# Two gate/up weight pairs instead of one take the two token halves apart in a SwiGLU channel mixer

## The chip, the cores and the metric

One core of one Trainium2 chip runs the whole program. Its engines are PE (matrix products), DVE (VectorE), ACT (ScalarE), POOL (GpSimd) and SP, which here only issues DMAs. The metric is device time in microseconds. Three runs of the kernel before took 3117.2, 3121.27 and 3121.76 us; the median is 3121.27.

## The reference

Two layers of a trunk run on 1152 tokens (128 context and 1024 sample tokens) of width 1024. Each layer is a token mixer followed by a dense SwiGLU channel mixer of hidden width 2816, both with adaptive scale, shift and gate:

```python
xs = xs + g1 * _token_mixer(_modulate(_rmsnorm(xs, norm1_g), sh1, sc1), ...)
xs = xs + g2 * _swiglu(_modulate(_rmsnorm(xs, norm2_g), sh2, sc2), w_gate, w_up, w_down)

def _swiglu(h, w_gate, w_up, w_down):
    return (jax.nn.silu(h @ w_gate) * (h @ w_up)) @ w_down
```

All of it is fp32. The change is in the channel mixer alone.

## The kernel before

Every fp32 product is made of three PE products of split operands: `hilo` (L212, L213) copies a tile to a rounded high part on ACT and subtracts it on POOL to get the low part; `mm3` (L227 to L229) multiplies high by high, high by low and low by high.

Gate and up products use a seven-product scheme on 2 x 2 blocks. The hidden width has 22 row tiles of 128, taken in 11 pairs; a pair has a gate and an up weight block. `gate_up` does one block with one half of the tokens (576 tokens in two columns of 288). Call that a **pass**: seven products of 12 matmuls of 128x288 each, in the order A11, A12, S2, S1, S3, S4, A22, with their sums on DVE (L1426). `prep_unit` readies the seven weight operands of a block: four loads of 256 KB (L204), and in the order A11, A12, A22, S1, S3, S2, S4 seven **splits** (a cast on ACT and a subtraction on POOL of 128x512 each), with four additions on DVE in between (L187, L190, L193, L196). The third product of a pass so needs the sixth split.

The tokens' operand is made by `half_apply` for one half at a time, in four **blocks**. In a block DVE scales eight or four column pieces (L1389), ACT adds the shift, DVE forms four differences `ht` (L1397 to L1400), ACT and POOL split them into `hth` and `htl` (one POOL subtraction of 128x1152), and ACT and DVE split the plain operands into `hx`, `hy`, `hz` (L1410, L1411). Half a (the later tokens) is ready when the mixer starts. Half b is not: its four blocks are done beside the first passes.

For that the first weight pair is taken with half a alone, the ten others with a and then b, and the first pair once more at the very end with half b alone, its weights loaded and split again. `units` in `mixer` is this list; `hidden` goes through it. In it, `prep[i][1]` is the making of the present weights, `nxt` that of the next block's, one step after most products (seven steps in seven products where a unit has one half), and `side` is work beside it: `half_apply` of half b in the first unit, with a block after the third and the sixth product of each pass, and `g_load` of the first tiles for the down projection in the last one. When a pass of `up` is done DVE multiplies it into the gate's result (L1482) and SP writes it to DRAM (`gd`). `DOWN` lists in which groups of row tiles the down projection reads them back.

The engines' orders come from a scheduler that is given the code in this order; each engine runs its own list in order, and waits for others by semaphores. The products sit in eight PSUM buffers.

Of the kernel before, what the change touches and what calls it, by code (L numbers as in the profile page):

```python
# [34 lines left out]
NH = 8  # L35
HID = 22
NP = HID // 2
DOWN = ((2, 3, 4, 5, 6), (7, 8, 9, 10, 11), (12, 13, 14, 15), (16, 17, 18, 19, 20), (21, 0, 1))
CORD = (2, 1, 0)
EPS = 1e-6  # L40
SCALE = 96.0 ** -0.5
# [35 lines left out]
class Net:  # L77
# [39 lines left out]
    def order(self):  # L117
        q = []
        for l in range(L):
            q += [("in", l, i) for i in range(len(IN_FM))]  # L120
            q += [("woa", l, m) for m in range(8)] + [("wob", l, j) for j in range(2)]
            q += [("wo", l, m) for m in range(8)]
            q += [("dn", l, g, m) for g in list(range(len(DOWN))) + [len(DOWN) - 1] for m in range(KD)]
        self.queue = q
        self.qpos = 0

    def wsrc(self, key):
# [10 lines left out]
        if k == "dn":  # L138
            n = len(DOWN[key[2]]) * P
            c = sum(map(len, DOWN[:key[2]])) * KD * P + key[3] * n  # L140
            return a["w_down"][l, :, c:c + n], n
# [1309 lines left out]
    def hidden(self, l, hs, units, prep, beside, gd):  # L1451

        nc = self.nc
        prods = [(u, n) for u in range(len(units)) for n in ("gate", "up")]
        g = {}
        for i, (u, n) in enumerate(prods):
            p, halves = units[u]
            W, nxt = prep[i][0], prep[i + 1][1] if i + 1 < len(prods) else iter(())  # L1460
            side = beside.get(u, iter(()))
            t = 0
            for _ in prep[i][1]:
                pass
            next(nxt, None)
            for H in halves:
                for o in self.gate_up(W, hs[H], i == 0):
                    if o is not None:
                        break
                    t += 1  # L1470
                    if len(halves) == 1 or t not in (1, 3, 6, 8, 10, 12, 14):
                        next(nxt, None)
                    if t % 3 == 0 or u:
                        next(side, None)
                if n == "gate":
                    nc.scalar.activation(o, o, AF.Silu)
                    g[H] = o
                    continue
                v = g.pop(H)
                for jj in range(2):  # L1480
                    s = slice(2 * jj, 2 * jj + 2)
                    nc.vector.tensor_tensor(v[:, s], v[:, s], o[:, s], op=ALU.mult)  # L1482
                if p not in gd:
                    gd[p] = self.tc.dram_tile([P, 2, T], F32, name=self._nm("gd"))
                if H == 0:
                    w = v.rearrange("p (j c) n -> p j c n", j=2)
                    for t0, n0, p0 in ((0, 64, 0), (128, 224, 64)):
                        for jj in range(2):
                            d = gd[p][:, jj, t0:t0 + 2 * n0].rearrange("p (c n) -> p c n", c=2)
                            nc.sync.dma_start(out=d, in_=w[:, jj, :, p0:p0 + n0])  # L1490
                else:
                    nc.sync.dma_start(out=gd[p][:, :, 576:1152], in_=v.rearrange("p (j c) n -> p j (c n)", j=2))
            if n == "up":
                for _ in side:
                    pass
            if i == len(prods) - 2:
                self.prep_next()
# [14 lines left out]
    def down(self, l, x, xd, gd, first, out):  # L1512

        g = first
        for gi in range(len(DOWN) - 1):
            nxt = []
            ld = self.g_load(gd, DOWN[gi + 1], nxt, ())
            for m in range(KD):
# [14 lines left out]
        def tail():  # L1533
            for cs in (CORD[:1], CORD[1:]):
                for m in range(KD):
                    w = self.get(("dn", l, len(DOWN) - 1, m), ahead=1 if cs[0] == CORD[0] or m < KD - 2 else 0)
                    for c in cs:
# [14 lines left out]
    def mixer(self, l, x, o_tail):  # L1552


        a, b = HORDER
        sa, sb = [], []
        for _ in zip(o_tail(a), self.half_sq(x, a, sa)):
            pass
        hs = {a: [], b: []}
        qb = self.half_sq(x, b, sb)  # L1560
        units = [(0, (a,))] + [(p, (a, b)) for p in range(1, NP)] + [(0, (b,))]
        prep = []
        for p, _ in units:
            for n in ("gate", "up"):
                W = {}
                prep.append((W, self.prep_unit(l, n, p, W)))
        ga = None
        for m, _ in enumerate(o_tail(b)):
            next(prep[0][1], None)
            if m == 0:  # L1570
                ya = self.half_rsq(a, sa)
                ga = self.half_apply(l, x, a, ya, hs[a])
            else:
                next(ga, None)
            next(qb)
        for _ in qb:
            pass
        yb = self.half_rsq(b, sb)
        xd = self.tc.dram_tile([P, KD, T], F32, name=self._nm("xmid"))
        for k in range(KD):  # L1580
            self.nc.sync.dma_start(out=xd[:, k, :], in_=x[k])
        gd = {}
        first = []
        ld = self.g_load(gd, DOWN[0], first, CORD)
        self.hidden(l, hs, units, prep, {0: self.half_apply(l, x, b, yb, hs[b]), len(units) - 1: ld}, gd)
        x = [self.S("x") for _ in range(KD)]
        if l + 1 < L:
            self.side = self.ada_work(l + 1, range(3))
        return x, self.down(l, x, xd, gd, first, self.o["yT"] if l == L - 1 else None)
# [197 lines left out]
```

## Time and profile before

| | before |
|---|---|
| median of three runs | 3121.27 us |
| the profiled execution | 3115.68 us |
| its span, first to last instruction | 3113.8 us |
| mean granted TensorE clock | 0.987 |
| PE busy | 97% |
| DVE / POOL / ACT busy | 55% / 38% / 36% |

A span of 3113.8 us lies within the 3115.68 us of that execution; 1.9 us lie around it. The busy shares are means over stages. Tables by stretch show where PE is not full, and lists of waits show what ended each idle time. PEclk is the granted clock as a share of 2.4 GHz; 0.50 is 1.2 GHz.

### The profile page before, as it was taken

The numbers are of one execution on the slowest core, as the hardware profiler recorded it, in microseconds if no ns is written. First come the engines' busy times: TensorE is split into PE (matmuls) and PEld (weight loads), VectorE is DVE, ScalarE is ACT, GpSimd is POOL, SyncE is SP. The second block draws the span as 40 slices with busy tenths as digits, with TensorE's granted clock in tenths as the row PEclk, the third lists the DMA queues.
The fourth block names the chain that finished last, engine by engine and source line by source line (L and its number), as shares of the span: only waits on it lengthen the run. The fifth ranks groups of instructions, "written<-read, shape, count | busy, mean of one in ns | idle before, by whom it ended". The sixth has DMA issues, their size and how long they took to land.

```text
span 3113.8 us, 48728 instructions
## 1 busy us (share of the span) xinstructions
PE 3016.3 (97%) x19136; PEld 2678.3 (86%) x19136; DVE 1708.1 (55%) x3315; ACT 1131.7 (36%) x2734; POOL 1185.4 (38%) x780
## 2 busy tenths in 40 slices
PE   6999999999799999999999999999988999999999
PEld 5989855569799999988999897554888999999999
DVE  6264467658855455643272645667578555556343
ACT  4334465444422222321153335654444222223211
POOL 3111254565644343311242113445656343434212
PEclk9999999999899999999999999999999999999999
DMA  5323000032222222566231110011232122216223
GB/s 214 103 88 132 25 17 30 32 117 99 79 85 72 69 73 86 192 245 239 65 115 49 46 36 13 13 54 59 73 129 68 60 85 83 68 63 234 92 71 100
DMA packets 126725, 278.06 MB, mean 89 GB/s; under 512 B 24096, under 2 KB 47392, under 8 KB 126496
## 3 DMA queue, kind: packets, MB, share of 16 engines
q1 hardware_dynamic: 126496, 274.95, 26.1%
q8 instruction: 151, 2.47, 0.3%
q14 instruction: 78, 0.64, 0.1%
HBM read 222.57 MB, written 52.33 MB: 88 GB/s over the span
## 4 chain that ended last, share of the span: by engine, by line
PE 85%; DVE 9%; ACT 2%; DMA 2%; issue 1%; POOL 1%; SPq 0%; DVEq 0%; POOLq 0%; ACTq 0%
PE mm L227 14%; PE mm L229 14%; PE mm L228 14%; PE ax L227 6%; PE ax L228 6%; PE ax L229 6%; PE ax L1136 5%; PE ax L1107 3%; PE mm L1153 2%; PE mm L1154 2%; PE mm L1155 2%; PE ax L325 1%; PE ax L1096 1%; DVE hb L1389 1%; DVE hy L1411 1%
## 5 line engine op out<-in xcount | busy, mean ns | idle before, releaser
L213 POOL TENSOR_TENSOR W<-r,W 128x512 fp32r<-128x512 f32 x336 | 448.9, 1348 | 539.3 <-ACT W L212 524.4
L213 POOL TENSOR_TENSOR W<-W,W 128x640 fp32r<-128x640 f32 (+5 forms) x168 | 297.9, 1775 | 841.4 <-ACT W L212 496.2
L227 PE MATMUL mm<-gh,W 128*128 128x384 f32 x1056 | 354.7, 336 | 1.4 <-DVE u L1426 1.3
L229 PE MATMUL mm<-gh,W 128*128 128x384 f32 x1056 | 353.4, 335 | 0.9 <-POOL W L213 0.9
L228 PE MATMUL mm<-gl,W 128*128 128x384 f32 x1056 | 352.9, 334 | 0.0
L1271 DVE SCALAR_TENSOR_TENSOR x<-mm,mod,x 128x128 f32<-128x128 f32 (+2 forms) x320 | 158.1, 515 | 332.5 <-PE mm L229 332.5
L229 PE MATMUL ax<-hth,W 128*128 128x288 f32 x1056 | 315.5, 299 | 10.3 <-POOL W L213 10.3
L227 PE MATMUL ax<-hth,W 128*128 128x288 f32 x1056 | 315.5, 299 | 7.4 <-ACT W L212 7.4
L228 PE MATMUL ax<-htl,W 128*128 128x288 f32 x1056 | 314.8, 298 | 0.0
L1145 POOL TENSOR_TENSOR W<-W,W 128x1024 f32<-128x1024 f32 x96 | 232.5, 2422 | 169.9 <-ACT W L1156 163.5
L212 ACT CAST W<-W 128x640 fp32r<-128x640 f32 (+5 forms) x168 | 131.6, 784 | 388.8 <-DMA W<-in_w_down 176.1
L212 ACT CAST W<-r 128x512 fp32r<-128x512 f32 x336 | 205.4, 621 | 183.8 <-DMA r<-in_w_up 64.2
L1109 DVE TENSOR_REDUCE mx<-ax 128x1 f32<-128x384 f32 x384 | 194.4, 550 | 120.4 <-PE ax L1107 119.1
L227 PE MATMUL mm<-hh,W 128*128 128x384 f32 x704 | 239.8, 341 | 0.0
L229 PE MATMUL mm<-hh,W 128*128 128x384 f32 x704 | 238.6, 339 | 0.0
L1156 ACT ACTIVATE W<-mm 128x512 f32<-128x512 f32 x288 | 168.2, 606 | 191.1 <-PE mm L1155 187.4
L228 PE MATMUL mm<-hl,W 128*128 128x384 f32 x704 | 237.0, 337 | 0.0
L229 PEld LDWEIGHTS ax<-hth,W 128*128 128x128 f32 x1056 | 201.9, 191 | 11.4 <-POOL W L213 11.4
L227 PEld LDWEIGHTS ax<-hth,W 128*128 128x128 f32 x1056 | 201.8, 191 | 8.3 <-ACT W L212 8.3
L227 PEld LDWEIGHTS mm<-gh,W 128*128 128x128 f32 x1056 | 198.2, 188 | 12.2 <-issue 10.1
L1136 PE MATMUL ax<-W,vt 128*64 128x512 f32 x576 | 206.8, 620 | 0.0
L228 PEld LDWEIGHTS ax<-htl,W 128*128 128x128 f32 x1056 | 201.9, 191 | 0.0
(335 smaller groups left out, 7789.5 us busy)
## 6 DMA issues: line engine op xcount, KB each, us to landing
W<-in_ada_w SPq DMA_DIRECT2D x80, 512.0 KB, 5.0
gr<-gd SPq DMA_DIRECT2D x44, 576.0 KB, 5.3
r<-in_w_gate SPq DMA_DIRECT2D x96, 256.0 KB, 2.9
r<-in_w_up SPq DMA_DIRECT2D x96, 256.0 KB, 4.1
W<-in_w_in_fm SPq DMA_DIRECT2D x30, 512.0 KB, 3.7
W<-in_w_down SPq DMA_DIRECT2D x48, 320.0 KB, 3.5
gd<-gu SPq DMA_DIRECT2D x22, 576.0 KB, 3.7
gd<-gu SPq DMA_DIRECT2D x44, 224.0 KB, 2.2
```

What stands on the lines that cost most here:

```text
L212: self.nc.scalar.copy(hi, raw)
L213: self.nc.gpsimd.tensor_tensor(lo, raw, hi.bitcast(F32), op=ALU.subtract)
L227: self.nc.tensor.matmul(ps, wh, xh, start=first and i == 0, stop=False)
L228: self.nc.tensor.matmul(ps, wh, xl, start=False, stop=False)
L229: self.nc.tensor.matmul(ps, wl, xh, start=False, stop=last and i == n - 1)
L1107: nc.tensor.matmul(ps, qh[0:96, qt * P:(qt + 1) * P], kh[0:96, c * CH:(c + 1) * CH], start=True, stop=True)
L1109: nc.vector.reduce_max(mx[:, qt, c:c + 1], ps, axis=AX.X)
L1136: nc.tensor.matmul(po[64 * qc:64 * qc + 64, :], vv[:, kt, b:b + 64], prs[kt][:, qs], start=(kt == 0), stop=(kt == 8))
L1145: nc.gpsimd.tensor_tensor(acc, acc, prs[kt], op=ALU.add)
L1153: nc.tensor.matmul(ps, kh[0:104, ks], qh[0:104, qs], start=True, stop=False)
L1156: nc.scalar.activation(pr[:, qs], ps, AF.Exp, scale=SCALE)
L1271: self.nc.vector.scalar_tensor_tensor(x[m][:, t0:t1], ps[:, t0 - c * CH:t1 - c * CH], self.mod[l][:, j, m, i:i + 1], x[m][:, t0:t1], ALU.m ...
```

## The change

The second pair of row tiles is treated like the first: half a alone at the beginning, half b alone at the end. The mixer then has two single-half units at either end instead of one. The blocks of `half_apply` for half b are spread over both first units: one after the third product of each of the four passes, instead of two in each of two passes. `DOWN` is rearranged so that the tiles which are finished last are read last.

```diff
-DOWN = ((2, 3, 4, 5, 6), (7, 8, 9, 10, 11), (12, 13, 14, 15), (16, 17, 18, 19, 20), (21, 0, 1))
+DOWN = ((4, 5, 6, 7, 8), (9, 10, 11, 12, 13), (14, 15, 16, 17), (18, 19, 20, 21, 2), (3, 0, 1))
...
-                    if t % 3 == 0 or u:
+                    if t == 3 or u > 1:
                         next(side, None)
...
-            if n == "up":
+            if n == "up" and beside.get(u + 1) is not side:
                 for _ in side:
                     pass
...
-        units = [(0, (a,))] + [(p, (a, b)) for p in range(1, NP)] + [(0, (b,))]
+        units = [(0, (a,)), (1, (a,))] + [(p, (a, b)) for p in range(2, NP)] + [(0, (b,)), (1, (b,))]
...
+        late = self.half_apply(l, x, b, yb, hs[b])
         first = []
         ld = self.g_load(gd, DOWN[0], first, CORD)
-        self.hidden(l, hs, units, prep, {0: self.half_apply(l, x, b, yb, hs[b]), len(units) - 1: ld}, gd)
+        self.hidden(l, hs, units, prep, {0: late, 1: late, len(units) - 1: ld}, gd)
```

What this does to POOL's list in layer 0: here is the kernel before, from the second pass of the first unit on. `htl` is the subtraction of a block of half b, `W` a split of weights (the `r` that it reads is a weight load).

```order
L213 TENSOR_TENSOR htl_7553<-ht_7547,hth_7552 128x1152
L213 TENSOR_TENSOR W_7682<-r_7581,W_7682 128x512
L213 TENSOR_TENSOR W_7701<-r_7580,W_7701 128x512
L213 TENSOR_TENSOR htl_7660<-ht_7654,hth_7659 128x1152
L213 TENSOR_TENSOR W_7719<-r_7581,W_7719 128x512
L213 TENSOR_TENSOR W_7763<-r_7579,W_7763 128x512
L213 TENSOR_TENSOR W_7809<-r_7770,W_7809 128x512
L213 TENSOR_TENSOR W_7840<-r_7771,W_7840 128x512
L213 TENSOR_TENSOR W_7858<-r_7773,W_7858 128x512
L213 TENSOR_TENSOR htl_7742<-ht_7736,hth_7741 128x1152
```

And this is the changed kernel from the same (second) block of half b on.

```order
L213 TENSOR_TENSOR htl_7634<-ht_7628,hth_7633 128x1152
L213 TENSOR_TENSOR W_7692<-r_7555,W_7692 128x512
L213 TENSOR_TENSOR W_7710<-r_7553,W_7710 128x512
L213 TENSOR_TENSOR W_7742<-r_7717,W_7742 128x512
L213 TENSOR_TENSOR W_7759<-r_7718,W_7759 128x512
L213 TENSOR_TENSOR W_7776<-r_7720,W_7776 128x512
L213 TENSOR_TENSOR W_7821<-r_7720,W_7821 128x512
L213 TENSOR_TENSOR htl_7799<-ht_7793,hth_7798 128x1152
L213 TENSOR_TENSOR W_7840<-r_7719,W_7840 128x512
L213 TENSOR_TENSOR W_7858<-r_7720,W_7858 128x512
L213 TENSOR_TENSOR W_7876<-r_7718,W_7876 128x512
L213 TENSOR_TENSOR W_7905<-r_7880,W_7905 128x512
```

Before, two and five splits stand between the second, third and fourth `htl`; now six stand between the second and the third, and seven (not all shown) between the third and the fourth: one whole weight block per block of tokens.

At the other end of the mixer, this is SP's list in the kernel before, at the last two-half pair; `r` are weight loads, `gd` writes of finished halves, `gr` reads for the down projection.

```order
L1492 DMA gd_12509<-gu_12152 256x1x576
L1504 DMA gr_12658<-gd_8135 128x1152
L204 DMA r_12630<-in_w_up 128x512
L204 DMA r_12631<-in_w_up 128x512
L204 DMA r_12632<-in_w_up 128x512
L204 DMA r_12633<-in_w_up 128x512
L1490 DMA gd_12509<-gu_12269 128x2x64
```

The changed kernel has at that place the following, from the last write of that pair's half b on.

```order
L1490 DMA gd_12298<-gu_12058 128x2x224
L204 DMA r_12555<-in_w_gate 128x512
L204 DMA r_12556<-in_w_gate 128x512
L204 DMA r_12557<-in_w_gate 128x512
L204 DMA r_12558<-in_w_gate 128x512
L1504 DMA gr_12724<-gd_8410 128x1152
L204 DMA r_12696<-in_w_up 128x512
L204 DMA r_12697<-in_w_up 128x512
```

The loads of the additional pair (gate, then up) stand behind that pair's writes, and the first read for the down projection stands between them.

## Rows read from the trace of the kernel before

**Rows 1.** The page: PE's busy time; a group's count, busy us, mean ns
```profile
PE 3016.3 (97%) x19136; PEld 2678.3 (86%) x19136; DVE 1708.1 (55%) x3315; ACT 1131.7 (36%) x2734; POOL 1185.4 (38%) x780
...
L212 ACT CAST W<-r 128x512 fp32r<-128x512 f32 x336 | 205.4, 621 | 183.8 <-DMA r<-in_w_up 64.2
```

**Rows 2.** Busy time by stretch; columns in the first line
```profile
core 0: us, PE busy (x) PEld busy (x) DVE busy (x) ACT busy (x) POOL busy (x), PEclk, DMA share, GB/s
775.00:850.00 75.00, 57.62 (x368) 55.86 (x367) 66.11 (x137) 37.57 (x64) 50.19 (x32) 0.84 0.26 88
1000.00:1200.00 200.00, 200.00 (x1508) 200.00 (x1507) 102.92 (x180) 54.62 (x90) 80.59 (x64) 1.00 0.24 79
2300.00:2400.00 100.00, 83.24 (x556) 81.29 (x556) 85.04 (x168) 48.21 (x81) 64.69 (x39) 0.88 0.21 73
```

**Rows 3.** PE's waits, 770 to 860 us: total us, times, longest
```profile
PE ax L249 <- DVE sq L416: 6.7, 1, 6.7
PE ax L229 <- POOL W L213: 5.6, 2, 2.9
PE ax L227 <- ACT W L212: 3.8, 2, 3.2
PE mm L228 <- DVE hz L1411: 1.0, 1, 1.0
```

**Rows 4.** PE's waits in layer 1, 2290 to 2400 us
```profile
PE ax L229 <- POOL W L213: 4.7, 2, 2.7
PE ax L227 <- ACT W L212: 3.6, 2, 3.2
```

**Rows 5.** PE in order of time: start, duration, [idle before, releaser]
```profile
807.59 0.61 PE L229 MATMUL ax<-hth,W 128*128 128x288 f32 x1 [2.68 <-POOL W L213]
...
829.96 0.61 PE L229 MATMUL ax<-hth,W 128*128 128x288 f32 x1 [2.88 <-POOL W L213]
...
842.48 0.40 PE L228 MATMUL mm<-hz,W 128*128 128x288 f32 x1 [1.01 <-DVE hz L1411]
```

**Rows 6.** Busy time by stretch, around half b's blocks
```profile
804.00:812.80 8.80, 5.88 (x25) 5.65 (x26) 8.80 (x14) 6.14 (x12) 8.80 (x6) 0.64 0.27 90
...
822.70:833.00 10.30, 4.27 (x19) 4.00 (x20) 10.30 (x19) 6.23 (x12) 7.58 (x4) 0.70 0.08 27
795.00:846.00 51.00, 40.65 (x267) 39.46 (x267) 50.48 (x89) 29.90 (x49) 38.00 (x22) 0.87 0.16 54
```

**Rows 7.** ACT: first product of two successive passes taken over
```profile
862.62 0.40 ACT L1429 COPY u<-ax 128x288 f32<-128x288 f32 x1 [6.88 <-PE ax L229]
...
873.78 0.40 ACT L1429 COPY u<-ax 128x288 f32<-128x288 f32 x1 [3.32 <-PE ax L229]
```

**Rows 8.** DVE and POOL by line, 1000 to 1200 us: busy us, mean ns
```profile
L193 DVE TENSOR_TENSOR r<-r,r 128x512 f32<-128x512 f32 x9 | 15.9, 1768 | 15.6 <-POOL W L213 15.6
...
L196 DVE TENSOR_TENSOR r<-r,r 128x512 f32<-128x512 f32 x9 | 6.1, 679 | 0.0
...
L213 POOL TENSOR_TENSOR W<-r,W 128x512 fp32r<-128x512 f32 x64 | 82.8, 1304 | 119.5 <-ACT W L212 115.9 <-DMA r<-in_w_up 1.7 <-POOL W L213 1.2
```

**Rows 9.** By tile, whole span: duration ns min/median/max
```profile
L213 POOL TENSOR_TENSOR htl<-ht,hth x16: 2657/2835/3210, 743.6 to 2377.7; 128x1152 fp32r<-128x1152 f32 x16
...
L1399 DVE TENSOR_TENSOR ht<-hb x16: 444/446/2655, 740.6 to 2375.6; 128x288 f32<-128x288 f32 x16
...
L1482 DVE TENSOR_TENSOR gu<-gu,gu x88: 746/758/2833, 826.0 to 2839.1; 128x576 f32<-128x576 f32 x88
```

**Rows 10.** End of the mixer: SP, POOL and PE in order of time
```profile
1265.31 2.41 SPq L204 DMA_DIRECT2D r<-in_w_up  x4
1274.19 2.64 SPq L1490 DMA_DIRECT2D gd<-gu  x4
...
1282.37 2.65 POOL L213 TENSOR_TENSOR W<-r,W 128x512 fp32r<-128x512 f32 x2 [1.28 <-ACT W L212]
...
1296.81 0.42 PE L227 MATMUL mm<-gh,W 128*128 128x384 f32 x1 [0.64 <-DVE u L1426]
```

## The prediction

> **What bounds the kernel now.** Start with the page: PE is busy for 97% of the span [rows 1], so a change that adds no PE work can only fill PE's idle times or make new ones. The table by stretch shows where they are. In the middle of the channel mixer PE is busy for 200.00 of 200 us at the full clock; at its start it has 57.62 of 75 us at a granted clock of 0.84 in layer 0, and 83.24 of 100 at 0.88 in layer 1 [rows 2]. PE's list of waits for that start tells what ended each one [rows 3]. 6.7 us is for the norm of half b, which stands ahead of the first pass and is not touched. 5.6 + 3.8 us is for splits of weights and 1.0 for half b's last plain operand, together 10.4 us in layer 0; layer 1 has 4.7 + 3.6 us for splits [rows 4]. So about 20 us of waits are aimed at.
>
> In order of time [rows 5] these fall behind each other: third product of the second pass at 807.59, third product of the third pass at 829.96, and half b's operand at 842.48. In the stretches with the two longer ones the clock is 0.64 and 0.70 on the mean [rows 6], so part of each ran at 1.2 GHz.
>
> Now who is late. From 795 to 846 us DVE is busy for 50.48 of 51 us and POOL for 38.00 [rows 6], while PE is not. Part of DVE's time is itself waiting: in the undisturbed middle, L193 takes 1768 ns and L196, of the same size, 679 [rows 8]. L193 starts when POOL goes from S1's split to S3's, and the additional 1.1 us is most of that 1.30 us split. L1399 of 444 ns took up to 2655, L1482 of 746 up to 2833 [rows 9]. A DVE operation on two SBUF tiles and a POOL split take turns here.
>
> **What the change removes and adds.** PE's products are the same in number and size. Removed is the crowding of two blocks of half b into each of two passes. Added are two weight blocks per layer (gate and up of the second pair, a second time), each four loads, seven splits and four DVE additions; and two of the first four passes' blocks must now be ready within one pass, not two.
>
> What is not removed: on DVE and POOL the order is the same up to the end of the first block, and the 807.59 wait ends with the split behind that block's `htl`. It stays, in both layers.
>
> I compare one mark: the start of the third product of the fifth pass, when as much PE work is done in both kernels. Before, the sixth pass's first product was taken over at 862.62 and the next one's at 873.78 [rows 7]; a pass is 11.16 us and a product 1.59, so the mark is 862.62 - 11.16 + 1.59 = 853.05.
>
> In the changed kernel the mark waits for the sixth split of the fifth pass's weights. Behind 807.59 POOL's order has until there 21 splits (one left of the second pass, seven, seven and six) and three `htl`: 21 x 1.30 + 3 x 2.66 = 35.3 us [rows 8, 9]. DVE has, on two SBUF tiles, 11 weight additions at 0.68 = 7.5, 12 `ht` at 0.445 = 5.3, two gate-by-up halves at 0.76 = 1.5, and the low parts of `hx`, `hy`, `hz`: by the sizes 0.45, 0.75, 1.05 and 0.45 = 2.7 [rows 8, 9] (the 864 columns by the slope between 288 and 576). That is 17.0, and 52.3 with POOL's.
>
> How strictly do they take turns? The same count for the kernel before from 807.59 to 842.48, that is 11 splits, three `htl`, 5 additions, 12 `ht`, the low parts with a second 576 piece, and the two halves, gives 22.3 + 13.7 = 36.0 us against 34.9 measured, 0.97. So 52.3 x 0.97 = 50.7, and the mark comes at 858.3: 5.2 us later.
>
> The Trainium skill, "SBUF — State Buffer", section "Who interferes with whom", states it as a rule: a DVE instruction with two inputs in SBUF contends with a GpSimd instruction that reads SBUF, and the one issued second is blocked until the first is done. Taken strictly (the 52.3 without a factor) that rule puts the mark at 859.9, 1.6 us beyond the measured share; it speaks against this change, since the change adds work of both kinds ahead of the mark.
>
> Following the handoffs one at a time with the same durations (DVE's in-order list, with its waits for PE's third product in each pass) I get the third pass's third product at about 823 instead of 829.96, the fourth's at 840 where before it was 842, and the mark at 855.5. The early gain is eaten because a pass with one block and one weight block takes POOL and DVE some 15 to 17 us and PE 11.16. Between 855.5 and 858.3 I take 857: **4 us later per layer**. Layer 1 has the same waits, so 8 us in all.
>
> Bounds. Below: if turns cost nothing, POOL's 35.3 us and per weight block the addition and cast of 0.69 + 0.62 us between A22 and S1 [rows 1, 8] make 807.59 + 35.3 + 3 x 1.31 = 846.8, 6.3 us sooner. Above: 858.3 and the same 3.9 is 862.2, and if PE is then at 1.2 GHz for 6 us, 3 us more (around 807.59 the mean of 0.64 over 8.8 us is 6.3 us at that level [rows 6]): 12 us later. For two layers that is -13 to +24.
>
> The end of the mixer I cost at nothing. One more single-half unit makes POOL's splits due every 11.16 us instead of every 22.3, 7 x 1.30 = 9.1 us of work. Before has one such pair of passes already and only 0.64 us of wait there [rows 10]. Cover: the loads of the additional pair stand behind four writes that took 2.64 us to issue at 1274.19; the earlier such loads at 1265.31 had their sixth split done by 1283.7 [rows 10], 18.4 us. From 1276.9 that is 1295.3, and it is needed two passes and two products after the pass that ended at about 1274, so at 1299.5. The cover is 4 us for gate and, since the next block's third load waits for a split of the block ahead, some 3 us for up. The new `DOWN` reads nothing that is not long written.
>
> **The sum.** Span 3113.8 + 8 = 3121.8; device time 3115.68 + 8 = 3123.7. The profiled execution is 5.6 us below the runs' median, so 3121.27 + 8 gives **3129**.
>
> **Rivals.** *Turns do not bind.* With half b's blocks apart, DVE's operations could fall into POOL's gaps. For it: POOL was idle for 13 of the 51 us [rows 6]. Against: the 0.97. In full it gives the lower bound, 6.3 us per layer, with up to 1.5 us of clock saved, 3106 to 3109; in part, up to 3115. *A wait for a wait.* The third pass's gain and the later loss cancel, mark at 851 to 855: 3117 to 3125. For it: the handoffs alone gave 855.5. *Late weights at the end.* If the last loads take 5 us longer than that cover was counted with, up's third product waits 2 us in either layer, and the clock may fall, 3 us more: 8 + 2 x (2 + 3) = +18, 3139. For it: the loads are behind the writes and a 576 KB read. It decides once the loads take over 3 us longer than at 1265. Against: before, the same pattern left 0.64 us.
>
> **Chances.** 0.2% is 6.2 us, about what a measurement of this kernel tells from none. My forecast's case (mark 855 to 862, +3 to +18) has 0.52, of which 0.17 lies under 6.2; turns that do not bind 0.17; a wait for a wait 0.20; late weights 0.11. So faster 0.17, same 0.37, slower 0.46. The range that holds 8 in 10 is 3113 to 3141: it leaves out the far part of the first rival and of the last.
>
> **What would show it.** Right: the 2.7 us wait at 807.59 unchanged; three waits for splits behind it, of 2 to 4 us, at third products of the third, fourth and fifth pass, where before were two and `hz`'s; no wait for `hz`; DVE over 95% busy for 45 us; no wait for splits over 1 us at the mixer's end. Wrong: waits for splits that sum to under 6 us per layer, with POOL's gaps filled and L1399 or L1482 at their shortest durations; or waits at the end.

## The result, and the profile after

The changed kernel takes 3148.37 us (median of 4 runs, 3147.44 to 3153.28) against 3120.12 us before: a ratio of 1.0095, 95% interval 1.0083 to 1.0106, so 28 us slower, clear of noise. Forecast were 3129 and a range up to 3141: the sign was right, the size was not. The profiled execution has a span of 3151.5 us.

First, the page, as in [rows 1]: PE, POOL's total, and the splits, which now come 28 times more.

```profile
PE 3035.3 (96%) x19136; PEld 2691.8 (85%) x19136; DVE 1731.5 (55%) x3331; ACT 1145.7 (36%) x2762; POOL 1222.7 (39%) x808
...
L212 ACT CAST W<-r 128x512 fp32r<-128x512 f32 x364 | 221.1, 621 | 221.8 <-DMA r<-in_w_up 65.2
```

Busy time by stretch, with columns as in [rows 2]: the middle is untouched; in the start PE is idle for 25 of 100 us in layer 0 and for 25 of 130 in layer 1.

```profile
775.00:875.00 100.00, 74.54 (x475) 72.16 (x473) 82.40 (x157) 45.20 (x79) 67.98 (x43) 0.86 0.24 83
1000.00:1200.00 200.00, 200.00 (x1508) 200.00 (x1507) 100.37 (x179) 55.58 (x91) 80.20 (x63) 1.00 0.22 72
2300.00:2430.00 130.00, 104.86 (x666) 102.48 (x665) 107.37 (x189) 58.98 (x99) 88.49 (x52) 0.84 0.25 86
```

PE's waits from 770 to 870 us, the answer to [rows 3]. Waits for POOL's splits went from 5.6 to 13.6 us; half b's last operand is no longer waited for; a wait for `x` of 3.3 us stands where before was 0.3, and that for half b's norm is 5.2 instead of 6.7.

```profile
PE ax L229 <- POOL W L213: 13.6, 4, 4.5
PE ax L249 <- DVE sq L416: 5.2, 1, 5.2
PE mm L227 <- DVE x L1317: 3.3, 2, 3.0
PE ax L227 <- ACT W L212: 3.3, 3, 1.4
```

The same in order of time, as in [rows 5], with the end of the mixer:

```profile
779.23 0.37 PE L227 MATMUL mm<-hx,W 128*128 128x288 f32 x1 [3.00 <-DVE x L1317]
...
809.87 0.41 PE L229 MATMUL ax<-hth,W 128*128 128x288 f32 x1 [2.69 <-POOL W L213]
...
827.05 0.61 PE L229 MATMUL ax<-hth,W 128*128 128x288 f32 x1 [2.76 <-POOL W L213]
...
846.57 0.61 PE L229 MATMUL ax<-hth,W 128*128 128x288 f32 x1 [4.51 <-POOL W L213]
...
864.01 0.40 PE L229 MATMUL ax<-hth,W 128*128 128x288 f32 x1 [3.61 <-POOL W L213]
...
1309.69 0.66 PE L227 MATMUL mm<-gh,W 128*128 128x384 f32 x1 [2.49 <-DVE u L1426]
```

PE runs 19136 instructions in both kernels, and only their order in the mixer differs, so the start times of the instruction with the same number can be set against each other. The table is worked out so. "x" is PE's 4200th to 4300th (13750th to 13900th in layer 1), which takes in the wait for `x` and that for half b's norm; "start" goes on to the 4760th (14380th), beyond the fifth pass's third product; "middle" to the 7900th (17500th); "end" to the 8060th (17660th). All in us. The changed kernel was run a second time later, and its two traces are both given.

| stretch | before, layers 0 and 1 | after, first trace | after, second trace | mean difference of a layer |
|---|---|---|---|---|
| x | 21.9, 30.7 | 24.9, 33.8 | 26.2, 32.6 | +3.1 |
| start | 78.9, 79.4 | 86.8, 91.8 | 88.5, 88.3 | +9.7 |
| middle | 417.2, 414.5 | 417.2, 414.5 | 417.2, 414.5 | 0.0 |
| end | 25.1, 26.5 | 28.3, 29.7 | 28.4, 29.7 | +3.2 |

That is 16.0 us a layer, 32 for both. The timed difference is 28.2; the kernel before's profiled execution lies 4.4 us below its median, which is about the rest. In the start, waits are 6.7 us of the 9.7 (16.8 against 10.1 on the mean). The clock makes the remaining 3: the granted clock was at its lower level, 1.2 GHz, for 22 us of that stretch on the mean, against 16 before.

### The profile page after: what moved, and what is told of

It is laid out like the page before. It is cut to its first block, busy times and chain, and to the rows that moved or that the text cites. A ratio compares the mean times of both kernels' runs of the same rounds, so it can differ in the third digit from the quotient of the medians.

```text
span 3151.5 us, 48878 instructions
## 1 busy us (share of the span) xinstructions
PE 3035.3 (96%) x19136; PEld 2691.8 (85%) x19136; DVE 1731.5 (55%) x3331; ACT 1145.7 (36%) x2762; POOL 1222.7 (39%) x808
## 3 DMA queue, kind: packets, MB, share of 16 engines
q1 hardware_dynamic: 128800, 279.14, 26.2%
## 5 line engine op out<-in xcount | busy, mean ns | idle before, releaser
L213 POOL TENSOR_TENSOR W<-r,W 128x512 fp32r<-128x512 f32 x364 | 486.0, 1351 | 529.9 <-ACT W L212 521.1
L212 ACT CAST W<-r 128x512 fp32r<-128x512 f32 x364 | 221.1, 621 | 221.8 <-DMA r<-in_w_up 65.2
L227 PEld LDWEIGHTS mm<-gh,W 128*128 128x128 f32 x1056 | 199.2, 189 | 16.6 <-issue 14.4
```

Of the source, the lines that this page charges most:

```text
L212: self.nc.scalar.copy(hi, raw)
L213: self.nc.gpsimd.tensor_tensor(lo, raw, hi.bitcast(F32), op=ALU.subtract)
L227: self.nc.tensor.matmul(ps, wh, xh, start=first and i == 0, stop=False)
```

## Experiments

Each was timed beside the kernel before on the same chip. The letters are the theories and rivals as the expectations name them. T: DVE's work on two SBUF tiles and POOL's work take turns, and their sum sets the start. L, P, B: a loop through the in-order queues sets it; they differ in the step they blame. D, Q: DVE's own in-order work sets it, whatever it waits for or reads.

**Half b's blocks put back, two in each of the first two passes** (the additional weight blocks stay):

```
-                    if t == 3 or u > 1:
+                    if t % 3 == 0 or u:
...
-            if n == "up" and beside.get(u + 1) is not side:
+            if n == "up":
...
-   {0: late, 1: late, len(units) - 1: ld}
+   {0: late, len(units) - 1: ld}
```

> The changed kernel with half b's four blocks back where they were, two in each of the first two passes. Theory L (a loop per pass, which no count of turns shows: POOL waits for S1's addition and cast, 1.46 us, then 3.1 to 3.4 us for the block's hth, then has htl and six splits; 17.5 us a pass against PE's 11.16): passes 3 to 5 then hold weights alone, 9.1 + 1.46 = 10.6 us each, so the waits at the third products of passes 4 and 5 (4.5 and 3.6 us) go, the mark (third product of the fifth pass) comes 8 us sooner in each layer, and only the wait of 2.3 to 2.5 us at the mixer's end stays: 3148 - 18 to 22 = 3126 to 3130. Theory T (the work on DVE and POOL that takes turns sets the mark, 52 us of it, wherever the blocks stand): the mark stays and the time is 3146 to 3150.

3141.88 us, ratio 1.0070 (1.0058 to 1.0083). The start takes 86.6 and 88.5 us, against 86.8 to 91.8 in the changed kernel: where the blocks stand is worth a microsecond or so, and L fell. The 6 us gained are mostly the wait for `x`, 0.8 us here and 0.3 in layer 1:

```profile
775.50 0.37 PE L227 MATMUL mm<-hx,W 128*128 128x288 f32 x1 [0.75 <-DVE x L1317]
```

So it is the additional weight blocks, and not the distribution of half b, that cost the start its time.

**The block after the first product, not the third:** `if t == 1 or u > 1`.

> The changed kernel with each block asked for after the first product of its pass, not the third; the same instructions, the block now ahead of S1's addition on DVE and htl ahead of S1's split on POOL. Theory L: hth is ready when htl's turn comes on POOL, the waits of 3.1 to 3.4 us for it go in three passes, so the waits at the third products of passes 4 and 5 fall from 4.5 and 3.6 to under 2 us: 3148 less 12 to 20 = 3128 to 3136. Theory T: the same 52 us of turns, 3146 to 3150.

3143.94 us, ratio 1.0074 (1.0061 to 1.0088); start 85.3 and 86.4 us. Between the two theories: PE now waits more for ACT's casts (8.5 us from 765 to 880) than for POOL's splits (4.0), and the start's waits shrank by 4 us a layer, where L wanted 6 to 10.

**`htl` of half b on DVE:**

```
-        self.nc.gpsimd.tensor_tensor(lo, raw, hi.bitcast(F32), op=ALU.subtract)
+        (eng or self.nc.gpsimd).tensor_tensor(lo, raw, hi.bitcast(F32), op=ALU.subtract)
...
```

The call for half b's `ht` then names VectorE as `eng`.

> The changed kernel with half b's htl on DVE instead of POOL (about 1.5 us for 2.66). Theory L: POOL's loop loses htl and the wait for hth, 3.1 + 3.3 us of 17.5 in each of three passes, 11.1 is left, as long as PE's pass: the split waits behind the 807.59 one fall under 1.5 us each, 3148 less 18 to 26 = 3122 to 3130. Theory T: 1.2 us of turns less for each of three blocks, 3.5 us a layer: 3139 to 3143.

3137.50 us, ratio 1.0059 (1.0047 to 1.0072); start 84.0 and 85.6, 4 us a layer less, as T had it (3.5), and a little more. L, which had 3122 to 3130, fell. From 807 to 861 us POOL was idle for 23 of 54 us, and PE still waited: taking `htl` off POOL did not cut the loop.

**Only the start doubled**, with the second pair's half b taken in the middle and one pair at the end; the order in which the down projection reads is the kernel before's again:

```
-DOWN = ((4, 5, 6, 7, 8), (9, 10, 11, 12, 13), (14, 15, 16, 17), (18, 19, 20, 21, 2), (3, 0, 1))
+DOWN = ((2, 3, 4, 5, 6), (7, 8, 9, 10, 11), (12, 13, 14, 15), (16, 17, 18, 19, 20), (21, 0, 1))
...
-  [(0, (a,)), (1, (a,))] + [(p, (a, b)) for p in range(2, NP)] + [(0, (b,)), (1, (b,))]
+  [(0, (a,)), (1, (a,))] + [(p, (a, b)) for p in range(2, 6)] + [(1, (b,))] \
+      + [(p, (a, b)) for p in range(6, NP)] + [(0, (b,))]
```

> The changed kernel's start, but the second pair's half b is taken in the middle of the mixer (between pair 5 and pair 6) and only the first pair's at the end, with the kernel before's order for the down projection. If the end's part of the loss is its own (the wait for the last evacuation grew from 0.6 to 2.5 and 2.3 us, with 3.4 us at the lower clock behind each), the wait is 0.6 again and the time is 3148 - 6.5 = 3141 to 3143. The rival: the end's wait has to do with the start's delay or with the other order of down, then 3147 to 3150.

3141.67 us, ratio 1.0070 (1.0056 to 1.0084). The end takes 25.4 and 26.9 us, 2.9 and 2.8 less than in the changed kernel, and its wait is 1.0 and 1.1 us. So the end's part does not come from the start's delay. Whether it is the second unit or the other order of reading, this run does not tell, since it puts both back; the new order alone does not make the wait, for with it and the additions regrouped (the next run) the end has none. The start, unedited here, takes 91.1 and 90.6 us with waits of 16.6 and 17.4, as in the changed kernel (16.6 to 16.9), but with 26 us at 1.2 GHz on the mean where that had 22: a start scatters by some 2 us through the clock.

**The weight additions regrouped**, so that the first is no longer written over `A22`, which POOL has yet to split, and the second no longer waits behind it; on the changed kernel, and on the kernel before (the comments are added here, and the rest of the edit, which moves S3's and S4's lines along, is left out):

```
         op("A12", b1)
+        V.tensor_tensor(a1, a1, a2, op=ALU.subtract)     # S3, over A11
         yield
         op("A22", b2)
-        V.tensor_tensor(b2, a2, b2, op=ALU.add)          # S1, over A22
+        V.tensor_tensor(a2, a2, b2, op=ALU.add)          # S1, over A21
         yield
-        op("S1", b2)
-        V.tensor_tensor(a2, a1, a2, op=ALU.subtract)
+        op("S1", a2)
+        V.tensor_tensor(b2, b2, a1, op=ALU.subtract)     # S2 = A22 - S3
...
```

> The changed kernel with the four weight additions regrouped: S3 = A11 - A21 goes over A11's tile and S1 = A21 + A22 over A21's, S2 = A22 - S3 over A22's; so the first two additions no longer wait for POOL's split of A22, only for that of A11, two splits earlier (2 x 1.35 us). Theory P (a loop through the in-order queues: L196's sum, ACT's four casts behind it, POOL's four splits up to A22's, L187 that writes over A22, then DVE's list from L187 to L196 with the block's operations in it; 17 to 18 us a pass): each pass of the loop is about 2.7 us shorter, the waits for splits behind the 807.59 one (13.6 us in layer 0) fall to 5 to 8, and with the clock the time is 3148 - 14 to 20 = 3128 to 3134. Rival D (DVE's own work, 47 of 54 us busy, sets the pass, in whatever order): the same work, 3145 to 3150.

> The kernel before with the same regrouping of the weight additions. Theory P: the waits for weights in the passes behind 807.59 (3.2 + 2.9 us in layer 0, 0.9 + 3.2 + 2.1 in layer 1) lose 2 to 3 us each where the loop turns once or twice: 3120 - 4 to 10 = 3110 to 3116, better than both kernels. Rival D: 3117 to 3123.

3123.09 us, ratio 1.0009 (1.0000 to 1.0018): 25 us off the changed kernel, 5 more than P's best, and D, for which the order did not matter (3145 to 3150), fell. And 3114.97 us on the kernel before, ratio 0.9984 (0.9975 to 0.9993): the fastest of all, better than both and as P had it; its one trace shows a start shorter by 1.4 and 0.5 us, an end shorter by 0.9 and 0.5 and a stretch "x" longer by 2.7 and 2.1, so where the 5 us lie is not shown. On the changed kernel P's places were wrong. In its start 7 us a layer went, 3.6 of them waits and most of the rest the clock's, but not at the third and fourth pass, where PE still waits 4.2 us for ACT's cast and 4.2 for POOL's split:

```profile
PE ax L229 <- POOL W L213: 7.1, 2, 4.2
PE ax L227 <- ACT W L212: 4.9, 2, 4.2
```

The third pass waits 7.1 us in all, where it was 4.1. What went is the 2.7 us wait of the second pass and that of the fifth (3.6, now 0.2), and the end has no wait at all (24.2 and 25.6 us, 4.1 less).

**The changed kernel again:**

> The changed kernel once more, unedited, for a second trace beside these: 3146 to 3151; the waits for splits at the third products of passes 3, 4 and 5 are 2.8, 4.5 and 3.4 to 3.7 us again in both layers, and the wait of 2.5 to 3.0 us for x ahead of half a's last product, which the kernel before didn't have, is there again if the changed order makes it, and may be absent if it is chance.

3147.53 us, ratio 1.0088 (1.0074 to 1.0101). The waits at the third products are 2.76, 4.51 and 3.53 in layer 0, and 2.76, 4.51 and 3.61 in layer 1; that for `x` is 4.2 and 3.0. All of it repeats.

**The block after the sixth product** (`if t == 6 or u > 1`), alone and with the regrouped additions:

> The changed kernel with each block asked for after the sixth product of its pass, not the third: DVE now has the four weight additions in front of the block, POOL has htl behind S2's split and not ahead of it. Theory B (the loop runs through the block: third product, its evacuation on DVE, the block's eight products with the norm, four ht, hth, htl, and only then S2's split, for which the next pass's third product waits; 17.4 to 19.5 us): that loop is cut; what is left is POOL's load of 7 splits, htl and S1's wait, about 13.6 us a pass against 11.16, for four passes, so the waits behind product two of the second pass fall from 16 us to 6 to 9 in each layer, and the time is 3148 - 12 to 22 = 3126 to 3136. Rival P (only the wait of L187 for A22's split counts, as theory P had it): that wait is as before, 3144 to 3150.

> Both edits on the changed kernel: the regrouped additions and the blocks after the sixth product. Theory B: the waits of 12.2 and 13.2 us that the regrouped version still has in passes 2 to 5 fall to 4 to 7, the mixer's end keeps no wait: 3123 - 8 to 16 = 3107 to 3115, the best of all. Rival P: the regrouping had taken all that the order of the additions gives, 3120 to 3126.

3136.32 us, ratio 1.0048 (1.0036 to 1.0061), and 3117.68 us, ratio 0.9995 (0.9986 to 1.0004). Both lie just beyond the slow edge of what B expected (3126 to 3136, 3107 to 3115), and the first far below P's 3144 to 3150. The start takes 82.5 and 84.0 us, and 78.6 and 80.0; the waits behind the second pass are still 13.1 and 10.5 us in layer 0, where B had 6 to 9 and 4 to 7. With B's loop cut, something else kept PE waiting.

**What it is: three doublings.** In each of half b's blocks one kind of work is done twice with the same values: `ht` on DVE (two SBUF tiles), `hb` on DVE (one operand in PSUM), `htl` on POOL.

```
+            for _ in range(1 if H == HORDER[0] else 2):      # ht: lines 1397 to 1400
+                        for _ in range(1 if H == HORDER[0] else 2):      # hb: line 1389
+            if H != HORDER[0]:                               # htl
+                nc.gpsimd.tensor_tensor(tl, t, th.bitcast(F32), op=ALU.subtract)
```

> The changed kernel with the four ht differences of each of half b's four blocks done twice (the same values): 1.5 us more DVE work on two SBUF tiles for each block, 5.9 us a layer. Theory T (turns: POOL's work and DVE's work on two SBUF tiles don't overlap, and their sum sets when the sixth pass can go; measured sum over elapsed 0.87 to 1.0): 5.9 / 0.9 = 6.5 us a layer, 3148 + 13 = 3159 to 3163. Theory Q (what counts is DVE's in-order list between two weight blocks, whatever its operands): the same, 3158 to 3162.

> The changed kernel with the eight products with the norm (L1389, one operand in PSUM) of each of half b's blocks done twice: 2.2 us more DVE work for each block, 8.8 us a layer, more than in the run with ht twice, but nothing of it on two SBUF tiles. Theory T: POOL goes on meanwhile, so the time stays within 4 us of 3148, up to 3154 with some of it on the path. Theory Q: 8.8 us a layer and the clock, 3164 to 3170.

> The changed kernel with htl of half b's blocks done twice on POOL: 2.62 us more for each block, 10.5 us a layer. Theory T: 10.5 / 0.9 = 11.7 us a layer, 3168 to 3174. Theory Q: POOL was idle for 13.6 of the 54 us up to the mark, so a part is absorbed, 3152 to 3162.

| doubled | added work, us a layer | start, us | longer by, mean of a layer | time, us |
|---|---|---|---|---|
| `hb`, PSUM operand, DVE | 8.8 | 90.4, 92.0 | 2.4 | 3150.70, ratio 1.0092 (1.0074 to 1.0109) |
| `ht`, two SBUF tiles, DVE | 5.9 | 93.2, 93.8 | 4.7 | 3152.23, ratio 1.0097 (1.0082 to 1.0112) |
| `htl`, POOL | 10.5 | 99.8, 101.6 | 11.9 | 3169.89, ratio 1.0154 (1.0139 to 1.0169) |

("Longer" is against 88.85, the mean of the changed kernel's two traces.) POOL's work is paid in full and a little over. DVE's work on two SBUF tiles is paid to four fifths, its work with a PSUM operand to a quarter at most; these two are rough, since such a start scatters by some 2 us through the clock. By PE's waits alone, which repeat better (16.6 to 17.4 us in the six layers with this start unedited), the three rows are longer by 0.7, 2.0 and 11.2 us. Q, for which every microsecond of DVE's list counts alike, would have had the first row at 3164 or more. T had the third row right (11.7) and the second too high (6.5, and 3159 to 3163 for the time). The run with `ht` twice has no wait for `x` (that stretch is 21.7 and 31.5 us, as in the kernel before), so it is only 4 us slower in all. With `htl` twice PE's waits for splits are, from 765 to 880 us:

```profile
PE ax L229 <- POOL W L213: 24.8, 4, 7.3
```

The durations in the changed kernel say which operand makes DVE wait. Of two operations of one size (ns, min/median/max), the one on two SBUF tiles is stretched to 2572 and the one with a PSUM operand never, though 77 of its 176 lay within POOL's instructions:

```profile
L1398 DVE TENSOR_TENSOR ht<-hb,ht x16: 442/452/2572, 741.2 to 2414.5; 128x288 f32<-128x288 f32 x16
...
L1426 DVE TENSOR_TENSOR u<-u,ax x176: 439/453/456, 796.5 to 2871.2; 128x288 f32<-128x288 f32 x176
```

**The floor.** Take about the shortest step between back-to-back starts as each operation's own duration (a split 1.27, `htl` 2.62, a weight addition 0.60, 288 columns on two SBUF tiles 0.37, 576 columns 0.72 and a half's gate by up 0.68; for 864 columns 1.06, an estimate by the slope of the others, since no run has them under 1.69), and add POOL's work in the start to DVE's work on two SBUF tiles:

| kernel | sum, layers 0 and 1 | start | sum over start |
|---|---|---|---|
| before | 68.5, 72.7 | 78.9, 79.4 | 0.87, 0.92 |
| changed | 77.0, 82.9 | 86.8, 91.8 | 0.89, 0.90 |
| additions regrouped | 77.0, 80.9 | 81.3, 82.7 | 0.95, 0.98 |
| regrouped, blocks late | 76.0, 80.0 | 78.6, 80.0 | 0.97, 1.00 |

The sums are good to some 2 us (a split's very shortest step is 1.22, and counting the operations at the edges otherwise moves a sum by about 1). No arrangement went below its sum; counted in much the same way the other runs lie between 0.86 and 0.97. The change adds 8.5 and 10.2 us to it, and the start became 7.9 and 12.4 us longer at almost the same ratio. What the orders change is the distance to the floor: 9 to 10 us in the changed kernel, 0 to 3 in the last row.

## Why the prediction was wrong

**Right.** What bounds the start, and by which resource; the wait of 2.7 us at 807.59, unchanged at 809.87; three waits for splits at the third products of the third, fourth and fifth pass, of 2.8, 4.5 and 3.6 us; no wait for `hz`; no wait for splits at the mixer's end; no gain from taking half b's blocks apart.

**The mark was mis-sized: +4 forecast, +8.7 measured** (9.1 on the mean of both layers and both traces, 6.6 of it waits and 2.5 the clock). From the 807.59 wait to the mark it took 864.01 - 809.87 = 54.1 us, against 45.5 before and the 49.4 that I took. The count of 52.3 us of turns was nearly right; I multiplied it by 0.97, leaned on a hand-off sequence that gave 48, and took a value between. The 0.97 was a wrong reading: I had counted with durations, and DVE's operations overlap (an `ht` lasts 0.45 us, and the next starts after 0.37). With the steps of the floor the same count is 33.9 of the 34.9 us before, and 49.4 of the 54.1 now: the stretch from which I took the share was full, and the new one is not. The share and the sequence both assume that, where one engine has no turn to take, the other always has. The trace of the changed kernel shows what happens instead. POOL in the fourth and fifth pass (start, duration, idle time before and what ended it):

```profile
834.98 1.29 POOL L213 TENSOR_TENSOR W<-r,W 128x512 fp32r<-128x512 f32 x1 [1.46 <-ACT W L212]
839.71 3.09 POOL L213 TENSOR_TENSOR htl<-ht,hth 128x1152 fp32r<-128x1152 f32 x1 [3.44 <-ACT hth L212]
842.76 8.70 POOL L213 TENSOR_TENSOR W<-r,W 128x512 fp32r<-128x512 f32 x6
852.92 1.34 POOL L213 TENSOR_TENSOR W<-r,W 128x512 fp32r<-128x512 f32 x1 [1.46 <-ACT W L212]
857.32 3.21 POOL L213 TENSOR_TENSOR htl<-ht,hth 128x1152 fp32r<-128x1152 f32 x1 [3.06 <-ACT hth L212]
```

and DVE in between:

```profile
833.55 0.69 DVE L187 TENSOR_TENSOR r<-r,r 128x512 f32<-128x512 f32 x1 [1.71 <-POOL W L213]
834.16 2.29 DVE L1389 SCALAR_TENSOR_TENSOR hb<-x,ab,ax 128x64 f32<-128x64 f32 x8
...
840.60 2.75 DVE L196 TENSOR_TENSOR r<-r,r 128x512 f32<-128x512 f32 x1
843.27 2.11 DVE L1411 TENSOR_TENSOR hy<-hb,hx 128x864 fp32r<-128x864 f32 x1
```

`L187` writes S1 over `A22`, so DVE waits for POOL's split of it (1.7 us), and POOL's next split waits for S1 (1.46 us). Then come 2.3 us of `hb`, with an operand in PSUM, four `ht` and ACT's cast to `hth`; POOL, whose split of S1 ends at 836.27, has nothing to do before that (3.4 us). And behind `hy` DVE's list holds the evacuation of the next third product, which waits for PE, which waits for POOL's split. POOL's two waits fall in each of the three passes, DVE's for the evacuation in two and its wait for the split of `A22` in one:

```profile
POOL htl L213 <- ACT hth L212: 8.5, 3, 3.4
POOL W L213 <- ACT W L212: 5.2, 3, 2.3
```

That they feed each other in a ring is read off the lists and not shown by a run of its own. The totals, first by stretch, for the kernel before and for the changed one:

```profile
807.00:842.00 35.00, 27.85 (x172) 27.12 (x172) 35.00 (x62) 21.30 (x37) 26.57 (x16) 0.81 0.16 54
```

```profile
809.00:864.00 55.00, 40.57 (x251) 39.41 (x251) 48.38 (x79) 29.18 (x51) 41.38 (x26) 0.84 0.21 69
```

and DVE's waits in the changed kernel's stretch:

```profile
DVE u L1426 <- PE ax L229: 4.3, 2, 3.1
DVE r L187 <- POOL W L213: 1.7, 1, 1.7
```

POOL is idle for a quarter of both stretches. But DVE was busy for all of the 35 us from which I took 0.97, and in the changed kernel it has 6.6 us of idle time in 55: with one block and one weight block in each pass DVE ran dry, and my count could not show it. I had it over 95% busy. The regrouping takes the link over `A22` out; since its waits went at other passes than this one, what that link alone cost stays open.

**The clock was left out of the likeliest case.** I had 3 us of it in the upper bound only. With more waits the granted clock stood at its lower level for longer (17 to 27 us at 1.2 GHz in the start, by trace and layer, against 14 to 18 before), which costs 3 us a layer, 2.5 of them ahead of the mark.

**The mixer's end cost 3.2 us a layer; I had nothing.** No split is late, as argued, and no load: ACT casts the last up block's first three operands back to back (1283.07, three in 1.66 us), and the split of `A22` ends only 0.2 us later against PE than before (0.5 in layer 1). What is late is DVE's list. While POOL splits those three, DVE does three parts for the down projection (L1509) and two products of gate by up; four of these five take 5.7 us where their shortest durations make 2.4. `L187` then starts without idle time, where before, in this layer, it waited for the split. First the changed kernel, then the kernel before:

```profile
1287.11 1.84 DVE L1482 TENSOR_TENSOR gu<-gu,gu 128x576 f32<-128x576 f32 x1
...
1289.35 0.76 DVE L1482 TENSOR_TENSOR gu<-gu,gu 128x576 f32<-128x576 f32 x1
1290.03 0.69 DVE L187 TENSOR_TENSOR r<-r,r 128x512 f32<-128x512 f32 x1
```

```profile
1277.12 0.69 DVE L187 TENSOR_TENSOR r<-r,r 128x512 f32<-128x512 f32 x1 [1.18 <-POOL W L213]
```

So the last weight block's additions stand 1.9 us later against PE (`L187` at 1290.03, 0.5 us behind the start of a product at 1289.52; before at 1277.12, 1.4 us ahead of the same one at 1278.49). DVE's parts for the down projection follow them, and the evacuation that frees PE's bank follows those. With one pair at the end and the old order of reading that is 1.0 us instead of 2.5, and with the regrouped additions, nothing. That the late `L187` makes PE's wait is read off the lists. "Late weights at the end" was among my rivals at 3139 and 0.11, with the split as what is late; the late thing is DVE's list.

**The stretch with the wait for `x` is 3.1 us a layer longer, and was on no list of mine.** DVE's and POOL's instructions are the same and in the same order up to there. What differs is who gets the turn. Before, at 755 us, and in the changed kernel, at 756 (`htl` runs on POOL from 755.22 and from 756.13):

```profile
755.71 2.85 DVE L414 TENSOR_TENSOR sq<-sq,sq 128x224 f32<-128x224 f32 x1
758.48 1.85 DVE L1411 TENSOR_TENSOR hz<-hb,hz 128x576 fp32r<-128x576 f32 x1
```

```profile
756.62 0.38 DVE L414 TENSOR_TENSOR sq<-sq,sq 128x224 f32<-128x224 f32 x1
756.94 3.21 DVE L1411 TENSOR_TENSOR hz<-hb,hz 128x576 fp32r<-128x576 f32 x1
```

`x` (L1317, at 775.30 and 778.46) starts 19.6 us behind that `sq` in the first pattern and 21.8 in the second: 2.2 of the 3.1 us; the rest fits the clock (11 us at 1.2 GHz in this stretch against 8 before, on the mean). Among the kernels with the old additions, the first pattern stands in both layers of three (before, blocks put back, `ht` twice), the second in both layers of the other seven, with the same 19.6 or 21.8 us to within 0.05. The changed kernel alone has two traces. Why a kernel falls on one side, with the same instructions ahead, stays open; nothing tried here tells it.

So the 4 us a layer of the forecast become 16: 5 more at the mark, half of them the clock's, 1 behind it, 3 at the end and 3 at `x`. Twice that is 32, and 28 less the 4 us by which the profiled execution of the kernel before lies under its median.

On the rule of the Trainium skill, "SBUF — State Buffer", section "Who interferes with whom", which I weighed against 0.97: taken strictly it gave a mark at 859.9, nearer to the measured one (861.7, with the 2.3 us that the changed kernel was late at 809.87 taken off) than mine. The same section says that a DVE instruction with at most one SBUF input, outside DVE's two-port modes, does not contend with GpSimd; the traces agree in kind: the operation with a PSUM operand took at most 456 ns beside POOL's work and the one on two SBUF tiles up to 2572, and the doublings cost 2.4 us for 8.8 of work with a PSUM operand and 4.7 for 5.9 on two SBUF tiles.

## What to carry to other kernels

Where two engines take turns, add up the work of both ahead of a mark and treat the sum as a floor: what a change adds to it is for the greater part paid, and a ratio under one from some other stretch is no discount. Then follow the in-order queues for the places where each engine waits for the other, and look first for an operation that overwrites a tile which the other engine has still to read; writing it over another tile took 25 us off here and 5 off the old kernel. When work is doubled at the beginning and at the end, cost the end by what stands behind it on every engine, not by the one transfer that might be late.

## What had not been expected of the hardware

The turn between DVE and POOL fell differently in kernels that run the same instructions up to there, the same way in both layers of each: 2.85 and 1.85 us for two operations in the one, 0.38 and 3.21 in the other, and `x`, for which PE waits, is 2.2 us later by it.
